# An encoder block's opening on one core: squares summed over channels by the tensor engine, first scale read from PSUM, last tile's products bank by bank

## Chip, cores, metric

One NeuronCore of a Trainium2 chip runs the whole program. The metric is device time in microseconds (us); lower is better. The engines are named as the profile names them: PE (tensor engine), ACT (scalar engine), DVE (vector engine), POOL (GpSimd), SP (the queue that issues most transfers).

## What is computed

One layer of a streaming-encoder block, x of 512 tokens by 1024 channels: a half-step SwiGLU FFN, a mixer (indexed sparse attention beside an RG-LRU branch), a second half-step FFN. Each sub-layer is RMSNorm, adaLN shift and scale from c, the sub-layer, RMSNorm, adaLN gate, residual. The change is in the first sub-layer's start:

```python
mod = (jax.nn.silu(c) @ w_ada[l] + b_ada[l]).reshape(B, N_MOD, D)
h = modulate(rmsnorm(x, ffn1_pre_g[l]), m[0], m[1])    # x * rsqrt(mean(x*x) + eps) * g, then h*(1+scale)+shift
y = swiglu(h, ffn1_w_gate[l], ffn1_w_up[l], ffn1_w_down[l])
x = x + 0.5 * m[2][:, None, :] * rmsnorm(y, ffn1_post_g[l])
```

## The kernel before

Activations stand transposed: channels on the 128 partitions, eight channel tiles of 128, and 512 tokens along the row. A weight W and an activation h are each split into a high part, rounded for PE's fast fp32 form, and a low remainder; a product is three matmuls per 128 channels (Whi·hhi, Whi·hlo, Wlo·hhi). `split` (L213) makes the parts: ACT copies the raw tile to hi (L217), DVE subtracts to lo (L221). Raw tiles come through a ring of three (`raw`), hi and lo through rings of six.

`start` (L511) is the opening. SP issues x in four transfers, the identity, then in turn the first adaLN weights (`wa`) and the first FFN weights (`w0`, one load for each of the eight channel tiles, each for three gate and three up column blocks). The order of PE's work in it is written out by hand (`manual_schedule`), and so is SP's order in the whole program; ACT, DVE and POOL, and PE outside the opening, follow a scheduler that simulates the program and issues what it holds to be ready.

- `busy(n)` (L571) puts n dummy 128x128 products of ones on PE.
- The sum of squares: ACT squares each tile of x (L620), DVE adds the eight (L624, L626) into one tile, PE sums its channels with four one-column matmuls (L630), ACT takes the root (L631), DVE the reciprocal (L632), PE spreads it over the partitions by four transposes (L636), and ACT copies that scale from PSUM to SBUF as `r` (L638).
- `mod_rows(g)` (L577) multiplies silu(c) by a group of adaLN weights, as rows of one partition (L585), `mod_cols(g)` (L589) turns the rows to columns (L594), adds the bias, and makes hi and lo of h for the tiles of the group (L603 to L605). `prepare(g)` (L607) splits the group's weights and makes u = x·r (L612).
- Then eight tiles k follow. For each, 18 products (L672) go to six PSUM banks (three gate, three up blocks): six Whi·hhi, six Wlo·hhi, six Whi·hlo. All six banks close in the last tile.
- `act_tile` (L675) makes silu(gate)·up: Silu on ACT (L679), product on DVE (L680), then hi and lo (L682, L683). The next weight tiles' products (L316 to L318) need the banks that it releases.

Four `mm` banks, two `wo` and two `aux` share PSUM. ACT loads a table set before a function that the present set lacks (ACT_TABLE_LOAD); `warm` (L562) is a one-element Sqrt that only loads the Sqrt set early. Later, `presplit` (L258) splits more weights in the background by way of POOL's transfers (L273 to L275), and `boundary` (L405) goes from one sub-layer to the next: `rstd_steps` (L321) sums squares on PE (L330), takes the reciprocal root on DVE by Newton steps (L336 to L348) or on ACT, and spreads it by transposes (L356); the second FFN then starts half by half of the tokens, with products at L310, L311 and L313 that take the low part of h last.

Of the kernel before, what the change touches and what calls it, by code (L numbers as in the profile page):

```python
# [9 lines left out]
AF = mybir.ActivationFunctionType  # L10
ALU = mybir.AluOpType
# [3 lines left out]
P = 128  # L15
S = 512
D = 1024
ND = D // P
# [14 lines left out]
NSTART = 3  # L33
# [77 lines left out]
class Build:  # L111
# [399 lines left out]
    def start(self):  # L511
        nc = self.nc
# [9 lines left out]
        w0 = [None] * ND  # L522
# [38 lines left out]
        warm = c.tile([P, 1], F32, name="warm")  # L561
# [9 lines left out]
        def busy(n):  # L571

            for _ in range(n):
                nc.tensor.matmul(idle[:, :P], self.ones, self.ones, start=True, stop=True)
# [14 lines left out]
        def mod_cols(g):  # L589

            pt = rows[g % 2]
            k0, n = groups[g][0], len(groups[g])
            for q in range(2 * n):
                nc.tensor.matmul(pt[:, q:q + 1], accs[g][:, q * P:(q + 1) * P], self.sel, start=True, stop=True)  # L594
            mk = self.modc[:, :16].rearrange("p (j d) -> p d j", d=8)[:, k0:k0 + n]
            bk = self.col("b_ada", 0, 16).rearrange("p (j d) -> p d j", d=8)[:, k0:k0 + n]
            nc.vector.tensor_tensor(mk, pt[:, :2 * n].rearrange("p (d j) -> p d j", j=2), bk, op=ALU.add)
            gm = self.modc[:, 8 + k0:8 + k0 + n]
            nc.vector.scalar_tensor_tensor(gm, gm, 1.0, self.col("g1pre", k0, n), op0=ALU.add, op1=ALU.mult)
            for k in groups[g]:  # L600
                gamma, beta = self.modc[:, 8 + k:9 + k], self.modc[:, k:k + 1]
                h32 = self.w2("h32")
                nc.scalar.activation(hi[k], us[k], AF.Identity, scale=gamma, bias=beta)  # L603
                nc.scalar.activation(h32, us[k], AF.Identity, scale=gamma, bias=beta)
                self.late = nc.vector.tensor_tensor(lo[k], h32, hi[k].bitcast(F32), op=ALU.subtract)  # L605

        def prepare(g):  # L607

            for k in groups[g]:
                self.split(w0[k])  # L610
                us[k] = self.w2("u")
                nc.vector.tensor_tensor(us[k], self.X[k], r, op=ALU.mult)  # L612

        with self.tc.manual_schedule(engines={mybir.EngineType.PE}):
            busy(34)

            totals = []
            for k in range(ND):
                sq = self.w2("sq")
                nc.scalar.activation(sq, self.X[k], AF.Square)  # L620
                if k < 2:
                    totals.append(sq)
                else:
                    nc.vector.tensor_tensor(totals[k % 2], totals[k % 2], sq, op=ALU.add)  # L624
            total = totals[0]
            nc.vector.tensor_tensor(total, total, totals[1], op=ALU.add)  # L626
            pt = self.bank("wo")
            s, s2 = [self.small.tile([P, 4], F32, name="s", tag="s4") for _ in range(2)]
            for q in range(4):
                nc.tensor.matmul(pt[:, q:q + 1], total[:, q * P:(q + 1) * P], self.ones[:, 0:1], start=True, stop=True)  # L630
            nc.scalar.activation(s, pt[:, :4], AF.Sqrt, bias=self.eps, scale=1.0 / D)  # L631
            nc.vector.reciprocal(s2, s)  # L632
            pb = self.bank("wo")
            mod_rows(0)
            for q in range(4):
                nc.tensor.transpose(pb[:, q * P:(q + 1) * P], s2[:, q:q + 1].to_broadcast([P, P]), self.ident)  # L636
            r = self.w2("r")
            nc.scalar.activation(r, pb, AF.Copy)  # L638
            prepare(0)
            mod_cols(0)  # L640
            mod_rows(1)
            busy(4)
            prepare(1)
            banks = [self.bank("mm") for _ in range(4)] + [self.bank("wo") for _ in range(2)]
            for gi, g in enumerate(groups):
                for k in g:
                    if k + 3 < ND:
                        fetch_w(k + 3)
                    if k < 2:
                        fetch(k + 3)  # L650
                    for part in range(3):
                        for j in range(2 * NSTART):
                            self.first_product(banks[j], w0[k], j, k, part)

                        if part == 0 and k == g[-1] and gi + 1 < len(groups):
                            mod_cols(gi + 1)
                    self.alive -= 1

                    if k == g[0]:
                        nx = gi + 2 if gi == 0 else gi + 1  # L660
                        if gi != 1 and nx < len(groups):
                            mod_rows(nx)
                            prepare(nx)
                    if k >= 6:
                        self.feed(k - 5)
# [728 lines left out]
```

## Time and profile before

| | |
|---|---|
| median of 3 runs | 1077.83 us (1075.47 to 1077.92) |
| the profiled execution | 1078.11 us, its span 1076.3 us |
| PE busy | 1047.9 us (97%) |
| DVE, ACT, POOL busy | 639.9 us, 481.5 us, 81.3 us |
| mean granted clock of PE | 0.984 |
| moved from and to HBM | 188.52 MB read, 23.61 MB written |

The span runs from the first to the last instruction; the execution's own time is 1.8 us longer. A granted clock of 1.00 is 2.4 GHz, 0.50 is 1.2 GHz. An fp32 matmul (dummies, sums, transposes) stands as two records in PE's rows, a product of split parts as one. In a timeline row the columns are start, duration, engine, line, operation, output<-input, tile sizes and the number of instructions merged; in brackets stands the engine's idle time before it and what ended that.

### The profile page before, as it was taken

How to read it: one execution, taken by the hardware profiler on the slowest of the kernel's cores; microseconds unless marked ns; L12 is line 12 of the kernel's file. 1: busy time of each engine (PE TensorE's matmuls, PEld its weight loads, DVE VectorE, ACT ScalarE, POOL GpSimd, SP SyncE). 2: the span in 40 equal slices, each digit the busy share in tenths (PEclk: the TensorE clock that was granted, in tenths of full speed). 3: DMA queues.
4: the chain of work that ended last, by engine and by line, in shares of the span. 5: the costliest groups of instructions: out<-in, count | busy, mean ns of one | idle time of the engine just before them, and what ended most of it. 6: DMA issues, size and time to landing. Idle time of an engine off the chain costs nothing.

```text
span 1076.3 us, 15177 instructions
## 1 busy us (share of the span) xinstructions
PE 1047.9 (97%) x5860; PEld 889.3 (83%) x5860; DVE 639.9 (59%) x1189; ACT 481.5 (45%) x779; POOL 81.3 (8%) x148
## 2 busy tenths in 40 slices
PE   8989999999999999999999999899999999999996
PEld 6778888878888999997776578899988888888895
DVE  4578578676866246479997555876423333333345
ACT  5564244333333356455876654554333222222252
POOL 0001111010111000000212410000000000000000
PEclk8999999999999999999999999899999999999998
DMA  9688898988989669583535412242433323333212
GB/s 369 262 329 288 296 350 308 335 287 305 369 296 369 236 218 336 205 325 117 200 128 168 149 42 79 79 138 88 148 118 98 93 86 100 114 98 98 98 41 79
DMA packets 56184, 211.03 MB, mean 196 GB/s; under 512 B 6936, under 2 KB 9304, under 8 KB 51504
## 3 DMA queue, kind: packets, MB, share of 16 engines
q1 hardware_dynamic: 42208, 161.72, 43.1%
q0 software_dynamic: 13904, 48.35, 12.6%
q8 instruction: 46, 0.75, 0.3%
q14 instruction: 26, 0.21, 0.1%
HBM read 188.52 MB, written 23.61 MB: 197 GB/s over the span
## 4 chain that ended last, share of the span: by engine, by line
PE 87%; DMA 5%; DVE 3%; ACT 3%; issue 2%; SPq 0%; DVEq 0%; ACTq 0%; POOLq 0%
PE mm L316 13%; PE mm L317 13%; PE mm L318 12%; PE wo L317 8%; PE wo L316 8%; PE wo L318 8%; PE mm L310 3%; PE mm L311 3%; PE mm L313 3%; DMA pre<-in_win_dram 2%; PE mm L1207 2%; PE wo L310 1%; PE wo L311 1%; PE wo L313 1%; PE aux L1244 1%
## 5 line engine op out<-in xcount | busy, mean ns | idle before, releaser
L217 ACT ACTIVATE hi<-raw 128x1024 fp32r<-128x1024 f32 (+2 forms) x192 | 196.8, 1029 | 304.6 <-PE mm L317 129.3
L221 DVE TENSOR_TENSOR lo<-raw,hi 128x1024 fp32r<-128x1024 f32 (+2 forms) x151 | 177.8, 1181 | 124.4 <-ACT hi L217 123.4
L316 PE MATMUL mm<-hhi,hi 128*128 128x512 f32 x368 | 144.9, 394 | 3.4 <-ACT sg L679 3.4
L318 PE MATMUL mm<-hhi,lo 128*128 128x512 f32 x368 | 143.8, 391 | 0.0
L317 PE MATMUL mm<-hlo,hi 128*128 128x512 f32 x368 | 143.7, 391 | 0.0
L316 PE MATMUL mm<-ahi,hi 128*128 128x256 f32 (+1 forms) x330 | 109.9, 334 | 1.0 <-ACT ahi L682 1.0
L316 PE MATMUL wo<-hhi,hi 128*128 128x512 f32 x280 | 110.0, 393 | 0.0
L317 PE MATMUL mm<-alo,hi 128*128 128x256 f32 (+1 forms) x330 | 109.9, 333 | 0.0
L318 PE MATMUL mm<-ahi,lo 128*128 128x256 f32 (+1 forms) x330 | 109.8, 333 | 0.0
L318 PE MATMUL wo<-hhi,lo 128*128 128x512 f32 x280 | 109.6, 391 | 0.0
L317 PE MATMUL wo<-hlo,hi 128*128 128x512 f32 x280 | 109.5, 391 | 0.0
L316 PEld LDWEIGHTS mm<-hhi,hi 128*128 128x128 f32 x368 | 69.5, 189 | 18.0 <-ACT sg L679 3.8
L318 PEld LDWEIGHTS mm<-hhi,lo 128*128 128x128 f32 x368 | 69.4, 189 | 14.6
L317 PEld LDWEIGHTS mm<-hlo,hi 128*128 128x128 f32 x368 | 69.6, 189 | 14.2
L456 DVE SCALAR_TENSOR_TENSOR macc<-wa,cs,macc 128x512 f32<-128x512 f32 x98 | 73.5, 750 | 5.2 <-DMA wa<-in_wa_dram 3.1
L273 ACT ACTIVATE pre<-pre 128x1024 fp32r<-128x1024 f32 x33 | 34.9, 1059 | 77.4 <-DMA pre<-in_win_dram 53.1
L316 PEld LDWEIGHTS mm<-ahi,hi 128*128 128x128 f32 x330 | 62.5, 190 | 7.4 <-ACT ahi L682 1.4
L317 PEld LDWEIGHTS mm<-alo,hi 128*128 128x128 f32 x330 | 62.7, 190 | 6.2 <-DVE alo L683 0.2
L318 PEld LDWEIGHTS mm<-ahi,lo 128*128 128x128 f32 x330 | 62.7, 190 | 6.0
L317 PEld LDWEIGHTS wo<-hlo,hi 128*128 128x128 f32 x280 | 52.6, 188 | 11.5 <-issue 0.7
L316 PEld LDWEIGHTS wo<-hhi,hi 128*128 128x128 f32 x280 | 52.6, 188 | 11.5 <-issue 0.5
L318 PEld LDWEIGHTS wo<-hhi,lo 128*128 128x128 f32 x280 | 52.6, 188 | 11.3 <-issue 0.5
(264 smaller groups left out, 2012.0 us busy)
## 6 DMA issues: line engine op xcount, KB each, us to landing
raw<-in_gu_dram SPq DMA_DIRECT2D x89, 512.0 KB, 3.6
wa<-in_wa_dram SPq DMA_DIRECT2D x36, 1024.0 KB, 10.0
lo<-pre SPq DMA_DIRECT2D x41, 512.0 KB, 5.2
pre<-pre POOLq DMA_DIRECT2D x33, 512.0 KB, 8.7
raw<-in_dn_dram SPq DMA_DIRECT2D x32, 448.0 KB, 3.5
raw<-in_win_dram SPq DMA_DIRECT2D x26, 512.0 KB, 5.7
raw<-in_dn_dram SPq DMA_DIRECT2D x22, 512.0 KB, 4.6
pre<-in_win_dram POOLq DMA_DIRECT2D x21, 512.0 KB, 5.0
```

The lines of the kernel that those rows point to most:

```text
L217: nc.scalar.activation(l.hi, l.raw, AF.Copy)
L221: nc.vector.tensor_tensor(l.lo, l.raw, l.hi.bitcast(F32), op=ALU.subtract)
L273: nc.scalar.activation(hi.bitcast(F32R), raw, AF.Copy)
L310: self.nc.tensor.matmul(ps, l.hi[:, kt], xh[kt][:, tok], start=(q == 0), stop=False)
L311: self.nc.tensor.matmul(ps, l.lo[:, kt], xh[kt][:, tok], start=False, stop=False)
L313: self.nc.tensor.matmul(ps, l.hi[:, kt], xl[kt][:, tok], start=False, stop=(q == n - 1))
L316: self.nc.tensor.matmul(ps, l.hi[:, kt], xh[kt][:, tok], start=(q == 0), stop=False)
L317: self.nc.tensor.matmul(ps, l.hi[:, kt], xl[kt][:, tok], start=False, stop=False)
L318: self.nc.tensor.matmul(ps, l.lo[:, kt], xh[kt][:, tok], start=False, stop=(q == n - 1))
L456: nc.vector.scalar_tensor_tensor(acc, w[:, k], ck, acc, op0=ALU.mult, op1=ALU.add)
L1207: nc.tensor.matmul(ps[:, :n], self.q[rows, g, i * P:(i + 1) * P], self.k[rows, g, :n], start=True, stop=False)
L1244: nc.tensor.matmul(ps[64 * e:64 * e + 64, :P], self.v[:, t, 64 * h:64 * h + 64], pts[e][:, t * P:(t + 1) * P], start=(t == 0), stop=(t == i))
```

## The change

The squares are no longer added by DVE: each squared tile goes to PE at once, which adds its channels into one PSUM column per 128 tokens over eight rounds, with four dummy products between rounds; the dummies ahead are 16 in place of 34. The first tile's u is made from the PSUM bank with the transposed scale, and the copy to `r` comes after it. In the last of the eight tiles all 18 products go bank by bank, three for each, and a one-element Silu stands ahead of them in the program.

```diff
         with self.tc.manual_schedule(engines={mybir.EngineType.PE}):
-            busy(34)
-
-            totals = []
+            busy(16)
+
+            pt = self.bank("wo")
             for k in range(ND):
                 sq = self.w2("sq")
                 nc.scalar.activation(sq, self.X[k], AF.Square)
-                if k < 2:
-                    totals.append(sq)
-                else:
-                    nc.vector.tensor_tensor(totals[k % 2], totals[k % 2], sq, op=ALU.add)
-            total = totals[0]
-            nc.vector.tensor_tensor(total, total, totals[1], op=ALU.add)
-            pt = self.bank("wo")
+                for q in range(4):
+
+                    nc.tensor.matmul(pt[:, q:q + 1], sq[:, q * P:(q + 1) * P], self.ones[:, 0:1],
+                                     start=(k == q == 0), stop=(k == ND - 1), skip_group_check=True)
+                if k < ND - 1:
+                    busy(4)
             s, s2 = [self.small.tile([P, 4], F32, name="s", tag="s4") for _ in range(2)]
-            for q in range(4):
-                nc.tensor.matmul(pt[:, q:q + 1], total[:, q * P:(q + 1) * P], self.ones[:, 0:1], start=True, stop=True)
             nc.scalar.activation(s, pt[:, :4], AF.Sqrt, bias=self.eps, scale=1.0 / D)
...
+            r = pb
+            prepare(0)
+            mod_cols(0)
             r = self.w2("r")
             nc.scalar.activation(r, pb, AF.Copy)
-            prepare(0)
-            mod_cols(0)
             mod_rows(1)
...
-                    for part in range(3):
+                    if k == ND - 1:
+
+                        nc.scalar.activation(warm, self.cs[:, 0:1], AF.Silu)
+                        for j in range(2 * NSTART):
+                            for part in range(3):
+                                self.first_product(banks[j], w0[k], j, k, part)
+                    for part in range(3 if k < ND - 1 else 0):
                         for j in range(2 * NSTART):
                             self.first_product(banks[j], w0[k], j, k, part)
```

Lines behind the opening move down by four (L679 is L683 in the changed kernel). What the scheduler makes of it shows in the order of the instructions. ACT's order from the first Silu on, before:

```order
L560 ACTIVATE cs<-cols 128x8
L562 ACT_TABLE_LOAD
L562 ACTIVATE warm<-cs,eps 128x1
L620 ACTIVATE sq<-X_116 128x512 x4
L620 ACTIVATE sq<-X_117 128x512 x4
L631 ACTIVATE s<-wo,eps 128x4
L217 ACTIVATE hi<-raw 128x768
```

and in the changed kernel:

```order
L560 ACTIVATE cs<-cols 128x8
L562 ACT_TABLE_LOAD
L562 ACTIVATE warm<-cs,eps 128x1
L651 ACT_TABLE_LOAD
L651 ACTIVATE warm<-cs 128x1
L620 ACTIVATE sq<-X_116 128x512 x4
L620 ACTIVATE sq<-X_117 128x512 x4
L217 ACTIVATE hi<-raw 128x768 x2
L628 ACT_TABLE_LOAD
L628 ACTIVATE s<-wo,eps 128x4
```

The one-element Silu (L651) stands ahead of the squares; two splits and a table load stand between the squares and the root (L628).

ACT's order at the end of the opening, from the last activations of h on (`lt` belongs to the decay branch of the mixer), before:

```order
L604 ACTIVATE h_514<-u,modc 128x512
L217 ACTIVATE hi<-raw 128x1024 x2
L273 ACTIVATE pre<-pre 128x1024
L982 ACT_TABLE_LOAD
L982 ACTIVATE lt_616<-lt_615 128x4
L217 ACTIVATE hi<-raw 128x1024 x2
L679 ACT_TABLE_LOAD
L679 ACTIVATE sg<-mm 128x512
```

and in the changed kernel:

```order
L604 ACTIVATE h_545<-u,modc 128x512
L217 ACTIVATE hi<-raw 128x1024 x2
L683 ACT_TABLE_LOAD
L683 ACTIVATE sg<-mm 128x512
L986 ACT_TABLE_LOAD
L986 ACTIVATE lt_648<-lt_647 128x4
L683 ACT_TABLE_LOAD
L683 ACTIVATE sg<-mm 128x512
L683 ACTIVATE sg<-wo 128x512
```

Two of the four splits (L217, 128x1024) have moved ahead of the last activations of h, and the decay branch's load now stands between the first and the second Silu.

PE's order in the second FFN, at the end of the first half of the tokens, where the root for the second half is made, before:

```order
L310 MATMUL wo<-hhi_6314,hi 128x256
L330 MATMUL aux<-ones,ssum 128x1 x4
L311 MATMUL wo<-hhi_6314,lo 128x256
...
L313 MATMUL wo<-hlo_6316,hi 128x256 x4
L313 MATMUL wo<-hlo_6317,hi 128x256 x4
L356 MATMUL aux<-ident,s 128x128 x2
L310 MATMUL mm<-hhi_6314,hi 128x256
```

and in the changed kernel:

```order
L311 MATMUL wo<-hhi_6347,lo 128x256
L313 MATMUL wo<-hlo_6348,hi 128x256 x4
L313 MATMUL wo<-hlo_6349,hi 128x256 x4
L330 MATMUL aux<-ones,ssum 128x1 x4
L356 MATMUL aux<-ident,s 128x128 x2
L310 MATMUL mm<-hhi_6346,hi 128x256
```

The sums (L330) stood 17 matmuls ahead of the transposes (L356), and now stand right in front of them.

## Rows read from the trace of the kernel before

**Rows 1.** The page's first part: busy us (share of the span), instructions.
```profile
PE 1047.9 (97%) x5860; PEld 889.3 (83%) x5860; DVE 639.9 (59%) x1189; ACT 481.5 (45%) x779; POOL 81.3 (8%) x148
```

**Rows 2.** Timeline of ACT, from 0 to 13 us.
```profile
4.27 0.29 ACT L562 ACTIVATE warm<-cs,eps 128x1 f32<-128x1 f32 x1
5.58 3.71 ACT L620 ACTIVATE sq<-X 128x512 f32<-128x512 f32 x6 [1.02 <-DMA X<-in_x_dram]
9.52 1.15 ACT L620 ACTIVATE sq<-X 128x512 f32<-128x512 f32 x2 [0.23 <-DVE sq L624]
```

**Rows 3.** Timeline of PE, from 12 to 27 us.
```profile
12.26 1.05 PE L630 MATMUL wo<-ones,sq 128*128 128x1 f32 x8 [1.83 <-DVE sq L626]
13.25 1.04 PE L585 MATMUL aux<-wa,cs 128*1 128x256 f32 x16
...
17.62 2.08 PE L574 MATMUL mm<-ones 128*128 128x128 f32 x8
19.34 2.05 PE L672 MATMUL mm<-hhi,hi 128*128 128x512 f32 x4
...
25.04 1.90 PE L585 MATMUL aux<-wa,cs 128*1 128x512 f32 x16
```

**Rows 4.** Windows of PE: stretch, length, PE busy (records), granted clock, DMA share, GB/s.
```profile
4.60:5.60 1.00, 1.00 (x12) 1.00 1.08 397
4.60:10.30 5.70, 5.70 (x53) 1.00 1.03 405
14.60:17.60 3.00, 3.00 (x23) 0.50 1.02 419
17.60:21.30 3.70, 3.70 (x17) 0.50 1.00 405
25.04:28.30 3.26, 3.26 (x23) 1.00 0.98 403
437.81:441.20 3.39, 2.45 (x20) 1.00 0.22 49
441.25:444.60 3.35, 3.35 (x16) 0.50 0.51 178
```

**Rows 5.** Timeline of PE at the end of the opening.
```profile
62.08 0.61 PE L672 MATMUL wo<-hlo,hi 128*128 128x512 f32 x2
66.12 0.80 PE L316 MATMUL mm<-hhi,hi 128*128 128x512 f32 x1 [3.42 <-ACT sg L679]
...
69.23 0.39 PE L317 MATMUL mm<-hlo,hi 128*128 128x512 f32 x1
...
71.50 0.39 PE L318 MATMUL mm<-hhi,lo 128*128 128x512 f32 x1
```

**Rows 6.** Timeline of ACT at the same place.
```profile
63.10 1.06 ACT L217 ACTIVATE hi<-raw 128x1024 fp32r<-128x1024 f32 x1 [2.15 <-DMA raw<-in_gu_dram]
64.17 1.28 ACT L679 ACT_TABLE_LOAD   x1
65.47 0.60 ACT L679 ACTIVATE sg<-mm 128x512 f32<-128x512 f32 x1
```

**Rows 7.** Timeline of PE in the second FFN.
```profile
724.96 0.95 PE L330 MATMUL aux<-ones,ssum 128*128 128x1 f32 x8
725.76 0.36 PE L311 MATMUL wo<-hhi,lo 128*128 128x256 f32 x1
...
729.17 0.41 PE L356 MATMUL aux<-ident,s 128*128 128x128 f32 x2 [1.13 <-DVE s L348]
```

**Rows 8.** DMA issues between 5.64 and 6.10 us: KB, us to landing.
```profile
raw<-in_w_dram SPq DMA_DIRECT2D x1, 384.0 KB, 10.9
```

**Rows 9.** Timeline of DVE in the second FFN.
```profile
725.94 0.16 DVE L336 TENSOR_SCALAR s<-aux 128x2 f32<-128x2 f32 x1 [1.98 <-PE aux L330]
...
728.87 0.16 DVE L348 SCALAR_TENSOR_TENSOR s<-s 128x2 f32<-128x2 f32 x1
```

**Rows 10.** Waits of PE over the span: us in total, times, longest.
```profile
PE mm L316 <- ACT ahi L682: 1.0, 1, 1.0
```

## The prediction

> **What bounds the kernel now.** I read the busy line of the page first. The tensor engine (PE) is busy for 97% of the span [rows 1], so time moves only where PE waits, runs at its lower clock, or does work that is no product. The change touches three such places, each read in the timelines of PE, ScalarE (ACT) and VectorE (DVE).
>
> The first is the opening. ACT squares the eight 128x512 tiles of x as their transfers land, from 5.58 to 10.67 us [rows 2]; DVE adds them up, and PE, idle for 1.83 us until it has, needs one set of four matmuls for the channel sums, from 12.26 to 13.31 [rows 3]. From there PE is the chain: adaLN rows, transposes and dummy products stand back to back until the first real product at 19.34, mostly at 1.2 GHz, the granted clock being 0.50 from 14.60 to 21.30 [rows 3, 4].
>
> The second is the end of the opening. The last product of the eight tiles starts near 62.3, and PE then stands idle for 3.42 us until the first Silu has released a bank; ACT was held by a split that waited for a weight transfer, and then by a 1.28 us table load [rows 5, 6]. After the gap PE runs at half speed until 69.2.
>
> The third is a place that the diff doesn't name: the middle of the second FFN's split half, where PE waits 1.13 us for the last reciprocal root [rows 7].
>
> **The change, part by part.**
>
> *Squares summed by PE.* DVE's seven adds go. In their place come 28 more one-column matmuls, in eight rounds of four, and dummy products of four between the rounds; the 34 dummies at the start become 16. Each fp32 matmul is two records. A dummy's record costs 0.112 us at 2.4 GHz (4.70 us more of window hold 41 more records, with one more at the edge, [rows 4]), a one-column record about the same, 8 being issued between 12.26 and 13.25, 0.12 each at most [rows 3]. So a round is 0.9 us and its dummies 0.9 us. All rounds and gaps together are 64 + 56 = 120 records, 13.4 us. ACT delivers a square every 0.6 us, so PE is the slower one, and the dummies, meant to bridge waits, come on the path.
>
> When can it begin? The order of ACT's instructions shows that the scheduler has put the new Silu load not ahead of the last tile but right behind the first Sqrt load. The Sqrt warm-up ends at 4.56 [rows 2]; a load of 1.28 and a short activation bring the first square to about 6.05, 0.5 later than now, and PE's first round to 6.7. PE's 16 dummies end near 6.3, so nothing else holds it. The sums are complete at 6.7 + 13.4 + 0.15 = 20.25 in place of 13.31: **+6.9**. Lower bound: at the 0.10 per record of the same kind of sum inside the product stream (8 records between 724.96 and 725.76, [rows 7]) the rounds shrink by 0.7, +6.2. Upper bound: everything at 1.2 GHz, where 8 records take 1.72 [rows 3], 25.8 in place of 13.4, +19.3. I take 2.4 GHz, because half of the mixed stretch is dummies: the stretch from 25.04 to 28.30, of which 1.9 us are one-row adaLN products and the rest real ones, kept clock 1.00, while the one from 437.81, with PE busy for 2.45 of 3.39 us, was followed by the lower clock [rows 3, 4].
>
> *New table load before the square root.* Silu's set being loaded, the Sqrt comes back with 1.28 us, behind two splits of weight tiles. The second tile lands about 16.6 (10.9 us after its issue at about 5.7) [rows 8], so split and load end near 18.8, before the sums at 20.25: nothing, as long as the squares are the later ones. If PE were done at 13.3 as now, this queue would cost 5 us.
>
> The load's price has a page in the Trainium skill, "ScalarE: Activation LUTs", section "What ACT_TABLE_LOAD costs": a load plus a drain, 2.66 us for each switch. The trace disagrees, its Silu starting 1.30 us after the load's start [rows 6]. By the page the squares and PE's rounds would begin 1.4 later, and the sum would be 1083.4.
>
> *First scale from PSUM, copy later.* DVE reads the transposes directly, and the copy (0.6 us, as the Silu of that size [rows 6]) goes behind the first tile's activations. PE's own chain is the bound between the sums and the first product, so I count nothing; the bank that the copy still reads is the sixth to be written, over a microsecond after the first. Bounds: -0.6 to +0.6, the copy itself either way.
>
> *The chain from sums to products* is as now, 6 us, with its stay at 1.2 GHz: when the rounds end, the same adaLN rows, transposes and one-column products follow. It shifts as a whole.
>
> *Last tile bank by bank.* The 18 products cost the same. The first bank closes 15 products, 3.4 us, before the last (0.227 each, ten starts from 69.23 to 71.50, [rows 5]). ACT's order now has the splits of the weight tiles earlier, so their ring slots and transfers come earlier; behind the last split stand a Silu load (the early one is lost to the Sqrt), the first Silu, a load for the decay branch, and Silu once more. Load and first Silu, 1.28 + 0.60 [rows 6], fit in the 3.4. The gap goes: 66.12 against 62.53, when the next product would have started, is **-3.6**; with no gap there is no lower clock, under which seven starts took 3.11 (66.12 to 69.23) where 1.59 is the normal price: **-1.5** [rows 5]. Bounds: -5.1, and 0 if the wait for the transfer at 63.06 stays. Late next are second and third Silu, whose banks PE wants 5 and 11 us later.
>
> *Second FFN.* The order shows PE's last channel sum of the mixer's boundary moved behind the last products of the first half, right in front of the transposes that need its root. Now 17 matmuls stand between, and cover 2.3 (725.76 to 728.04, which is 729.17 less 1.13) of the 3.1 us that DVE takes from reading the sums (725.94) to the last Newton step (729.03) [rows 7, 9]. In the changed order the products end 0.8 earlier, the sums at 728.2, the root near 731.2, and the transposes start at 731.3 against 729.17: **+2.1**. Bounds: +1.5 with nothing interleaved on DVE; +3.5 if the longer wait also lengthens the stay at 1.2 GHz.
>
> *Other queues.* SP's order is unchanged. On ACT, DVE and POOL the pre-split tiles of later weights change places with their neighbours; the products of the first FFN hide that now but for one wait of 1.0 us on PE [rows 10], and I leave it at nothing, between -1.0 and +1.0, should that wait go or come twice.
>
> Sum: 6.9 - 5.1 + 2.1 = +3.9 on the profiled execution's 1078.11 (span 1076.3 and 1.8 around it; it lies 0.3 above the median of 1077.83): **1082.0 us**. A difference under 0.3%, 3.2 us, can't be told from none here.
>
> **The rivals.**
>
> *A. The clock holds.* The new opening leaves PE hardly an idle moment until the first product. If only idle time lowers the clock, the 6.7 us at 1.2 GHz [rows 4] run at 2.4, and give back 3.35: 1078.6, not slower. Against it: PE showed no idle time between 12.26 and the fall at 14.6, and it stayed low to 17.60 though PE was busy throughout [rows 3, 4]. The Trainium skill's "TensorE: Matmul & The Clock Gate", section "Why this matters for your kernels", says this rule: leave no idle gaps between bursts of matmuls and the clock stays. The rows agree for the gap at 62.7, not for the second half of the first stay. Chance 0.15.
>
> *B. The clock falls amid the rounds.* From the middle of the rounds, near 13.4, the remaining 6.8 us then double: 1088.8; from 11 on it would be 1091. For it: the fall at 14.6 came behind such one-column matmuls; against it: the stretch at 25.04 [rows 3, 4]. Chance 0.17.
>
> *C. The gap stays.* If the last weight transfer is again late against the end of the products, ACT reaches its load late, and 1.5 to 5 us of the gain don't come: 1083.5 to 1087. It needs a landing after the first bank's closing; splits moved ahead speak against it. Chance 0.10.
>
> *D. The rounds hide.* If the weight loads of a round slip under the dummies' streaming, the two don't add, the rounds cost 13.4 - 6.3, and the sum is -2.4: 1075.7; with A as well 1072.4. For it: PE's loads overlap its matmuls. Against it: one-column records in a stream still took 0.10 each [rows 7]. Chance 0.13.
>
> **How the numbers follow.** The forecast holds 0.45, within 1080.5 to 1083.5; about 0.28 of it lies above the bound of 1081.06, 0.17 below. Slower: 0.28 + 0.17 (B) + 0.10 (C) = 0.55. Same: 0.17 + 0.13 of A + 0.06 of D = 0.36. Faster: 0.02 + 0.07 = 0.09. Range 1076.0 to 1089.0: it leaves out the lower half of D and the worse form of B. The likeliest case's own range is 1080.5 to 1083.5.
>
> **What would show it.** Sums right: the last one-column record of the opening ends near 20.2, the first product starts near 26.2. Right on the load: two table loads before the squares and one more before the root, PE never waiting for it. End: no gap between the last tile's products and the next weight tile, clock 1.00 there. Second FFN: an idle stretch of 3 us before the transposes in place of 1.13. The forecast is wrong if the sums end before 16 or after 24, or if the gap is still over a microsecond.

## The result, and the profile after

| | before | changed |
|---|---|---|
| median (runs) | 1076.65 us (4, 1070.96 to 1077.92) | 1089.68 us (4, 1089.49 to 1090.34) |
| the profiled execution, its span | 1078.11 us, 1076.3 | 1089.49 us, 1087.7 |

The changed kernel is slower: 1.0125 times, 95% interval 1.0093 to 1.0157, of which 1 is no part. Slower was forecast, but 1082.0 us, and 1089.68 lies just outside the range that ended at 1089.0. The spans differ by 11.4 us where +3.9 was expected, so 7.5 us came from somewhere else.

The busy line of the page after answers to [rows 1]: PE's share is the same 97%, and it is busy for 8.7 us longer.

```profile
PE 1056.6 (97%) x5934; PEld 898.8 (83%) x5936; DVE 636.1 (58%) x1182; ACT 485.2 (45%) x783; POOL 81.7 (8%) x148
```

**The opening, as far as the first product.** PE's timeline after, against [rows 3] (L623 are the sums, L574 the dummies, L676 the products that were L672):

```profile
7.08 0.95 PE L623 MATMUL wo<-ones,sq 128*128 128x1 f32 x8
7.89 1.14 PE L574 MATMUL mm<-ones 128*128 128x128 f32 x8
...
19.59 0.95 PE L623 MATMUL wo<-ones,sq 128*128 128x1 f32 x8
20.47 1.04 PE L585 MATMUL aux<-wa,cs 128*1 128x256 f32 x16
...
24.50 1.17 PE L676 MATMUL mm<-hhi,hi 128*128 128x512 f32 x4
```

The rounds and their dummies alternate without a gap, and the sums end at 20.54 (19.59 + 0.95) in place of 13.31, 7.2 later. But the first product comes 4.0 us after that, not 6.0: the adaLN rows and transposes ran at full clock. ACT's timeline, against [rows 2], shows the Silu load ahead of the squares and the Sqrt load back before the root, both hidden: the second load is done at 20.03, and the sums end at 20.54.

```profile
4.56 1.28 ACT L651 ACT_TABLE_LOAD   x1
...
5.96 3.21 ACT L620 ACTIVATE sq<-X 128x512 f32<-128x512 f32 x6
...
18.75 1.28 ACT L628 ACT_TABLE_LOAD   x1
20.58 0.26 ACT L628 ACTIVATE s<-wo,eps 128x4 f32<-128x4 f32 x1 [0.54 <-PE wo L623]
```

**Three places behind it.** PE's timeline after, at the last adaLN columns of the opening, at its end [rows 5], in the first FFN, and in the second [rows 7]:

```profile
57.80 1.87 PE L594 MATMUL aux<-sel,macc 128*128 128x1 f32 x8 [2.69 <-ACT macc L587]
...
72.44 0.39 PE L676 MATMUL wo<-hlo,hi 128*128 128x512 f32 x1
72.67 0.39 PE L316 MATMUL mm<-hhi,hi 128*128 128x512 f32 x1
...
244.90 0.73 PE L316 MATMUL mm<-ahi,hi 128*128 128x512 f32 x1 [4.01 <-ACT ahi L686]
...
739.13 0.40 PE L356 MATMUL aux<-ident,s 128*128 128x128 f32 x2 [2.89 <-DVE s L348]
```

At 72.67 the gap of 3.42 us is gone, as forecast. The other three are what to look at: a wait of 2.69 that did not exist, one of 4.01 where 0.97 stood (the 1.0 of [rows 10]), and 2.89 in place of 1.13. Windows of PE give the clock (columns as in [rows 4], but with all five engines' busy time ahead of it: PE, PEld, DVE, ACT, POOL):

```profile
6.00:20.54 14.54, 14.54 (x135) 14.53 (x137) 1.92 (x2) 7.36 (x12) 0.00 (x0) 1.00 1.02 412
20.54:24.50 3.96, 3.95 (x48) 2.39 (x49) 1.14 (x4) 1.98 (x4) 0.00 (x0) 1.00 1.04 419
...
57.27:64.09 6.82, 6.29 (x19) 5.33 (x20) 3.38 (x5) 4.20 (x6) 1.08 (x2) 0.50 1.00 371
...
245.00:248.41 3.41, 3.41 (x8) 2.65 (x9) 2.32 (x3) 1.23 (x2) 0.54 (x1) 0.50 0.81 290
...
739.93:746.76 6.83, 6.12 (x28) 6.12 (x29) 6.03 (x16) 3.34 (x8) 0.00 (x0) 0.50 0.01 2
```

Behind each of the three waits PE then works at 0.50 for a while. At 57 and at 245 it loses half of that stay, as it has work nearly throughout. In the second FFN it loses less, since part of the stay is idle time: run 6, further down, has the same stay of 6.8 us, run 5 has none, and the stay costs run 6 about 1.8 us. The difference of the spans is made up of these: first six products, +4.2 (the next record, the adaLN columns, starts at 25.98 against 21.74); wait and clock at 57, 2.7 + 3.4, +6.1; end of the opening, -5.1; wait and clock in the first FFN, 4.0 - 1.0 + 1.7, +4.7; a stay at 0.50 in the mixer that no longer occurs (the last of [rows 4]), -1.7; second FFN, +2.8 (the same products of PE start at 724.24 and 732.53 ahead of its wait, 8.3 later, and at 751.00 and 762.12 behind its stay, 11.1 later). Together +11.0, against 11.4; what is left is in small shifts, the largest one of 0.5 near 120 us.

**Where the new waits come from.** ACT copies `macc`, PE's adaLN rows, out of PSUM. ACT's timeline after:

```profile
56.20 1.06 ACT L273 ACTIVATE pre<-pre 128x1024 fp32r<-128x1024 f32 x1 [3.43 <-DMA pre<-in_dn_dram]
57.16 0.58 ACT L587 ACTIVATE macc<-aux 128x512 f32<-128x512 f32 x1
...
243.28 1.06 ACT L273 ACTIVATE pre<-pre 128x1024 fp32r<-128x1024 f32 x1 [7.99 <-DMA pre<-in_wv_dram]
244.24 0.61 ACT L686 ACTIVATE ahi<-a 128x512 fp32r<-128x512 f32 x1
```

Both times ACT stood in front of a pre-split copy (L273), waiting for POOL's transfer of that weight tile, and what PE wanted was queued right behind. The chain of waits runs through it (start, length, what):

```profile
46.48 3.60 DMA pre<-pre
...
50.10 0.02 POOLq L266
50.12 0.50 issue
...
50.63 5.46 DMA pre<-in_dn_dram
...
56.20 1.06 ACT pre L273
57.26 0.49 ACT macc L587
57.75 0.04 issue
57.80 1.87 PE aux L594 x8
```

In the kernel before a copy stood ahead of that `macc` too, but it was the second tile's. POOL had issued its load at 44.41, ahead of the first tile's write, and ACT waited 1.1 us for it, unseen by PE. Now the write goes first, and the copy ahead of `macc` is the third tile's (run 7 ties just this one). `presplit` has two buffers that it takes in turn, so the third tile's load goes to the buffer that the first tile's write reads. POOL's queue waits for that write, which lands at 50.08, and the load is issued at 50.63; the second tile's load comes right behind it. The x tiles in the other buffer came free at nearly the same time (50.04), but only the second tile's load needs them.

### The profile page after: what moved, and what is told of

Same layout as the page of the kernel before. It is cut to its first block, busy times and chain, and to the rows that moved or that the text cites. A ratio compares the mean times of both kernels' runs of the same rounds, so it can differ in the third digit from the quotient of the medians.

```text
span 1087.7 us, 15322 instructions
## 1 busy us (share of the span) xinstructions
PE 1056.6 (97%) x5934; PEld 898.8 (83%) x5936; DVE 636.1 (58%) x1182; ACT 485.2 (45%) x783; POOL 81.7 (8%) x148
## 4 chain that ended last, share of the span: by engine, by line
PE 79%; DMA 11%; DVE 4%; ACT 2%; issue 2%; DVEq 0%; POOL 0%; SPq 0%; ACTq 0%; POOLq 0%
PE mm L316 10%; PE mm L317 10%; PE mm L318 10%; PE wo L317 7%; PE wo L316 7%; PE wo L318 7%; DMA pre<-pre 5%; DMA pre<-in_win_dram 3%; PE mm L310 3%; PE mm L311 3%; PE mm L313 3%; PE mm L1211 2%; PE mm L676 1%; PE wo L310 1%; PE wo L311 1%
## 5 line engine op out<-in xcount | busy, mean ns | idle before, releaser
L217 ACT ACTIVATE hi<-raw 128x1024 fp32r<-128x1024 f32 (+2 forms) x192 | 197.0, 1029 | 292.2 <-PE mm L317 100.8
L316 PE MATMUL mm<-hhi,hi 128*128 128x512 f32 x368 | 144.1, 392 | 0.0
L316 PE MATMUL mm<-ahi,hi 128*128 128x256 f32 (+1 forms) x330 | 110.6, 336 | 4.0 <-ACT ahi L686 4.0
L316 PE MATMUL wo<-hhi,hi 128*128 128x512 f32 x280 | 109.9, 393 | 0.0
L318 PEld LDWEIGHTS mm<-hhi,lo 128*128 128x128 f32 x368 | 69.1, 188 | 14.6
L317 PEld LDWEIGHTS mm<-hlo,hi 128*128 128x128 f32 x368 | 69.1, 188 | 14.1
L316 PEld LDWEIGHTS mm<-hhi,hi 128*128 128x128 f32 x368 | 69.1, 188 | 14.0
L273 ACT ACTIVATE pre<-pre 128x1024 fp32r<-128x1024 f32 x33 | 34.9, 1059 | 92.7 <-DMA pre<-in_win_dram 46.5
L316 PEld LDWEIGHTS mm<-ahi,hi 128*128 128x128 f32 x330 | 62.8, 191 | 10.5 <-ACT ahi L686 4.4
L274 DVE TENSOR_TENSOR pre<-pre 128x1024 fp32r<-128x1024 f32 x33 | 40.3, 1223 | 41.0 <-ACT pre L273 41.0
L310 PE MATMUL mm<-hhi,hi 128*128 128x256 f32 x232 | 60.9, 294 | 1.2 <-ACT hhi L373 1.1
```

Source lines behind the costliest of these rows:

```text
L217: nc.scalar.activation(l.hi, l.raw, AF.Copy)
L273: nc.scalar.activation(hi.bitcast(F32R), raw, AF.Copy)
L274: nc.vector.tensor_tensor(raw.bitcast(F32R), raw, hi, op=ALU.subtract)
L310: self.nc.tensor.matmul(ps, l.hi[:, kt], xh[kt][:, tok], start=(q == 0), stop=False)
L316: self.nc.tensor.matmul(ps, l.hi[:, kt], xh[kt][:, tok], start=(q == 0), stop=False)
L317: self.nc.tensor.matmul(ps, l.hi[:, kt], xl[kt][:, tok], start=False, stop=False)
```

## Experiments

**The theory:** the loss beyond the rounds is the scheduler's new order, set off by the squares' edit: the pre-split's loads, writes and copies on POOL and ACT, and the sums in the second FFN. **Its rivals:** the waits come from the other parts (the scale in PSUM, the early Silu, bank by bank), or from PE's lateness or busy transfers, whatever the order.

The kernel before was run beside each group of runs; its median was 1076.0 to 1076.5 us beside runs 1 to 11. Single runs of one kernel differ by several us (those of the kernel before lay between 1068 and 1085), so the ratios carry the verdicts on time and the traces those on places. The table gives, for each profiled execution, how much later than in the kernel before (us) the same five records of PE start (the last one: ends): the first product, the first product of the next weight tile (L316, the end of the opening), the first product with `ahi` (first FFN's second weight), the first with `mhi` (end of the mixer), and PE's last record.

| | first product | next tile | first `ahi` | first `mhi` | last | ratio of times, interval |
|---|---|---|---|---|---|---|
| changed | +5.2 | +6.6 | +5.0 | +8.3 | +11.4 | 1.0125 (1.0093 to 1.0157) |
| 1 squares alone | +4.7 | +2.2 | +0.9 | +10.9 | +14.1 | 1.0150 (1.0114 to 1.0187) |
| 2 DVE squares | +0.1 | -1.8 | -3.2 | -3.7 | -3.7 | 0.9962 (0.9933 to 0.9990) |
| 3 pre-split held | +4.9 | +1.0 | -0.4 | +4.6 | +4.6 | 1.0086 (1.0058 to 1.0115) |
| 4 rounds bare | +5.4 | +2.3 | +0.9 | +5.4 | +5.9 | 1.0054 (1.0021 to 1.0087) |
| 5 40 dummies | -1.4 | -4.1 | -5.5 | -8.2 | -8.4 | 0.9953 (0.9931 to 0.9975) |
| 6 41 dummies | -1.2 | -4.6 | -6.0 | -6.1 | -4.6 | 0.9981 (0.9955 to 1.0008) |
| 7 one copy later | +5.0 | +6.6 | +5.1 | +7.3 | +5.3 | 1.0042 (1.0021 to 1.0063) |
| 8 one dummy | +4.7 | +1.7 | +0.3 | +0.6 | +3.4 | 1.0083 (1.0055 to 1.0111) |
| 9 dummies alone | -0.9 | -2.0 | -1.8 | -3.1 | -5.0 | 0.9983 (0.9962 to 1.0005) |
| 10 bank and dummies | +0.7 | -2.4 | -3.8 | -5.5 | -5.9 | 0.9969 (0.9941 to 0.9996) |
| 11 38 dummies | +1.1 | -2.6 | -4.0 | -7.0 | -6.9 | 0.9972 (0.9945 to 0.9998) |

**1. Squares alone.** The squares' part of the diff, put into the kernel before, and nothing else.

> The kernel before with one part of the change: squares summed by PE in eight rounds with dummies. Theory (the extra time comes from the squares' edit: the rounds on PE's path, and the new order that the scheduler makes of it; the other parts don't move the order): sums complete near 20.0, first product near 24.2 at full clock; the wait of PE for the copied adaLN rows (macc) near 56 comes as in the changed kernel, 2.7 us and 3.3 of lower clock behind it; the second FFN costs 3.5 as there; the end of the opening keeps a gap of 1 to 3.4 us. 1083 to 1092 us, likeliest 1088. Rival (the waits come from reading the scale in PSUM, the early Silu or the bank-by-bank tile): only the rounds cost, 1080 to 1081, and no macc wait.

Measured: 1092.63 us. The theory's cause holds, its place only in part. PE waited 1.07 us for `macc` with no lower clock behind it, but three times in the first FFN (2.9, 1.9 and 3.5 us, for `ahi` and `alo`; ahead of the first ACT had waited 5.7 us in a pre-split copy), with 10.2 us at 0.50; the second FFN has its 2.9 us. So the squares' edit alone brings about the whole loss (the two intervals overlap), in an order of its own. The rival's 1080 is excluded. Unexpected: the gap at the end of the opening shrank to 0.5 us without the bank-by-bank order, ACT having done the decay branch's load earlier. PE's products there go from 5.2 us late to 0.9 us late, so 4.3 of the 5.1 us come without that part of the change.

**2. The other parts without the squares.** The changed kernel with these lines back:

```diff
-            busy(16)
+            busy(34)
...
-                for q in range(4):
-                    nc.tensor.matmul(pt[:, q:q + 1], sq[:, q * P:(q + 1) * P], self.ones[:, 0:1],
-                                     start=(k == q == 0), stop=(k == ND - 1), skip_group_check=True)
-                if k < ND - 1:
-                    busy(4)
+                if k < 2:
+                    totals.append(sq)
+                else:
+                    nc.vector.tensor_tensor(totals[k % 2], totals[k % 2], sq, op=ALU.add)
...
```

> The changed kernel with the squares added by DVE again; PSUM scale, bank-by-bank tile and early Silu stay. Theory: the order behind the opening is that of the kernel before, so no macc wait, 1.0 us of wait at the first FFN, 1.1 in the second; the end of the opening gains its 5.1; two table loads more in the opening cost at most 0.5. 1071 to 1073.5 us, about 4.5 below the kernel before. Rival (these three parts bring the waits, or gain nothing): 1077 or more.

Measured: 1072.27 us, faster than both kernels, as the theory has it. POOL's order and PE's are those of the kernel before, no wait for `macc`, 1.13 us in the second FFN.

**3. The order alone, first way.** The changed kernel, with the first two pre-split copies of ACT tied behind its last activation of h (`self.h32` is that instruction, and `issue_after` puts what is written in its block behind it on the same engine):

```diff
-            nc.scalar.activation(hi.bitcast(F32R), raw, AF.Copy)
+            with self.tc.issue_after(self.h32.ins) if k < 2 else contextlib.nullcontext():
+                nc.scalar.activation(hi.bitcast(F32R), raw, AF.Copy)
```

> The changed kernel with one thing added: ACT's first two pre-split copies are ordered behind its last activation of the opening's h. Theory (ACT stood in a pre-split copy that waited for its transfer, with macc queued behind): the macc wait near 56 and the lower clock behind it go, -6.0; in the second FFN the sums stand 20 matmuls ahead of the transposes again, -3.5; the wait of 4 us near 241, of the same kind, may stay or go (-4.7). 1075 to 1081 us. Rival (PE late by the rounds, or the transfers' contention, makes those waits whatever the order): a wait of over a microsecond stays before the adaLN columns near 56, 1087 to 1091.

Measured: 1084.82 us, 1082.76 in the profiled execution. The rival falls: with PE just as late (+4.9 at the first product), no wait stands before the columns near 55, the clock is 1.00 from the rounds to 346 us, and the wait near 241 is down to 0.6. At the first `ahi` product the kernel is 0.4 ahead of the one before, where the changed kernel is 5.0 behind. The second FFN's wait is 1.1 again. But the time is above the expected range, since other waits come with the delayed pre-split (lines lie two lower here); the one at L492, which run 4 with the same copies held has too, is followed by 3.4 us at 0.50:

```profile
PE aux L492 <- DVE macc L458: 3.1, 1, 3.1
...
PE wo L318 <- ACT ahi L688: 1.9, 1, 1.9
```

**4. Rounds without dummies.** No `busy(4)` between the rounds, no early Silu, ACT's opening in program order, the copies held as in 3.

> The changed kernel without the dummies between the rounds and without the early Silu, ACT's opening in program order, the first two pre-split copies held as in the third run. Theory: PE's eight rounds of 0.9 us follow ACT's squares and end near 14.0, little later than DVE's way; if the clock holds from there to the first product, as it does in the changed kernel, 3 us less than before, with the end of the opening's 5.1: 1068 to 1071 us; if it falls as in the kernel before, 1071 to 1074. Rival (the dummies are what holds the clock): the lower clock lies over the adaLN rows as in the kernel before.

Measured: 1083.43 us; a miss on the opening, and the rival is right. Windows of this run, from the first round to the end of the sums (columns as above):

```profile
6.00:10.21 4.21, 4.21 (x37) 4.21 (x35) 0.00 (x0) 3.44 (x6) 0.00 (x0) 1.00 1.03 389
10.21:18.46 8.25, 8.25 (x41) 8.23 (x41) 0.00 (x0) 1.15 (x2) 0.00 (x0) 0.50 1.02 420
```

PE is busy throughout, with nothing but one-column sums from 7.42 on, and the clock falls at 10.21 and stays low until 23.87. The sums end at 18.5, 2 us earlier than with the dummies, and the first product is the latest of all. The dummies are not idle weight: with four of them between rounds the clock held in the rounds, in the changed kernel and in runs 1, 3 and 7, and without them it fell.

**5 and 6. Idle time, and one dummy more.** The kernel before with scale from PSUM and bank by bank, DVE's squares, and only the number of leading dummies changed:

```diff
-            busy(34)
+            busy(40)
```

(41 in run 6.)

> The kernel before with the first scale from PSUM and the last tile bank by bank, DVE adding the squares, no early Silu, and 40 dummies ahead in place of 34; the order of the other engines is that of the kernel before. PE's idle time ahead of the sums shrinks from 1.95 to about 0.6 us. Theory (that idle time let the clock fall at 14.6): the clock stays 1.00 to the first product, which starts near 16.4 in place of 19.4: 1068 to 1070 us. Rival (the one-column sums, one-row products and transposes let it fall, whatever came ahead): it falls near 14.6 again, first product at 19.4, 1071 to 1073 us as in the second run.

> The fifth run with one dummy product more, 0.22 us of PE's work in its idle time, by which the scheduler puts the second FFN's sums right ahead of their transposes and, in the opening, a weight split ahead of the root. Theory (the order alone makes the second FFN's loss): 2.9 us of wait in place of 1.1 there, and 6.8 us at the lower clock in place of 3.4, +3.5 against the fifth run, and 0.3 to 0.5 for the split: 3 to 4.5 us slower than the fifth. Rival (the loss comes with the late start of the changed kernel): the two agree within 1 us.

Measured: 1070.73 and 1074.44 us. Run 5 has the lowest ratio of all, 0.9953 of the kernel before, though the intervals of runs 2, 10 and 11 overlap its own. PE's timeline of run 5 shows no idle time ahead of the sums, and the first product 5.3 us after their start instead of 7.1:

```profile
1.01 11.74 PE L574 MATMUL mm<-ones 128*128 128x128 f32 x80 [1.01 <-POOL sel L555]
12.66 1.05 PE L630 MATMUL wo<-ones,sq 128*128 128x1 f32 x8
...
17.93 1.17 PE L677 MATMUL mm<-hhi,hi 128*128 128x512 f32 x4
```

The clock stays 1.00 until 661.7 us; the stays at the end of the opening, at 441 in the mixer and behind the 1.13 us of wait in the second FFN are gone with it. Run 6 adds one dummy of 0.2 us, and the second FFN's sums change place as in the changed kernel. The same line of PE's timeline, of run 5 and of run 6:

```profile
722.26 0.41 PE L356 MATMUL aux<-ident,s 128*128 128x128 f32 x2 [1.13 <-DVE s L348]
```

```profile
724.24 0.66 PE L356 MATMUL aux<-ident,s 128*128 128x128 f32 x2 [2.89 <-DVE s L348]
```

With it come 6.8 us at 0.50 (722.84 to 729.67), where run 5 has none: PE's transposes start 2.0 us later than in run 5, its products behind the stay 3.8 us later. From the last `mhi` product to the end run 6 loses 3.1 us against run 5 (1059.31 - 675.99 against 1063.13 - 676.69). No late start of PE is needed for that loss; a different order is enough. A further 2 us comes from a wait behind ACT in the first FFN, at 230.

**7. The order alone, second way.** The changed kernel with just the third tile's copy, the one ahead of `macc`, tied behind it (k == 2 and `macc` in place of k < 2 and `h32`).

> The changed kernel with one instruction ordered: ACT's pre-split copy of the third tile, which stood ahead of the last macc, has to follow it. Theory: the wait of 2.7 us near 55 and the 6.8 us of lower clock behind it go, -6.0; the second FFN's sums stand 21 matmuls ahead of the transposes again by the scheduler's new order, -3.5; two copies now stand ahead of the last four activations of h and may hold them for their transfers, 0 to 2 us; the wait of 4 us near 241 may stay or go. 1076 to 1083 us. Rival (late PE or busy transfers make the wait): over 1 us of wait stays at the adaLN columns near 55, 1087 or more.

Measured: 1081.66 us. The wait before the columns is gone, the second FFN is back at 1.1 us, and the time is in the range. But the two copies that now stand ahead of the last h hold PE there; the trace has it as (lines two lower):

```profile
PE mm L678 <- ACT hhi L605: 4.2, 1, 4.2
PE mm L318 <- ACT ahi L688: 3.4, 1, 3.4
```

0 to 2 us were expected, so this was underestimated: the wait moved to the next thing in ACT's queue, since the transfer itself is no earlier, and 3.4 us at 0.50 came with it. The 3.4 in the first FFN also stays.

**8. One dummy between rounds.** `busy(1)` for `busy(4)`, ACT's opening in program order, no early Silu, second and third copy held.

> The changed kernel with one dummy between the rounds in place of four, without the early Silu, ACT's opening in program order, the second and third pre-split copy held behind the opening's last activation. For the opening's clock: if a quarter of a microsecond of dummies in every 1.2 is enough, the clock stays at 1.00 and the sums end near 16.3, the first product near 20; if not, it falls amid the rounds as in the fourth run, sums near 20. The rest of the program as in the third and fourth runs, 1076 to 1084 us.

Measured: 1086.9 us (1081.53 profiled), above the range. The clock fell at 11.50, PE without a gap from 6.41 on, and the sums ended at 18.43. One dummy product in each round is not enough here; four were.

**9 to 11. Parts, once more.** Run 9 is the kernel before with 40 dummies and nothing else; run 10 adds the bank-by-bank tile, without the scale from PSUM; run 11 is run 5 with 38 dummies.

> The kernel before with 40 dummies ahead in place of 34, and nothing else. Theory (the fill holds the clock in the opening; only the last tile's bank-by-bank order closes the gap at the opening's end): no stay at 1.2 GHz from 14.6 to 21.4, first product 1.0 to 1.8 us earlier, but the gap of 3.4 us before the next weight tile stays within a microsecond, with its lower clock: 1073 to 1075 us. Rival (the gap goes when ACT and its transfers shift against PE, without the new order): 1071 or less.

> The fifth run without the scale read from PSUM: the copy to r comes first again, as in the kernel before. Theory (that scale is worth nothing, since PE's own chain is the bound there): within 0.7 us of the fifth run, 1070 to 1071.5. Rival (the copy of 0.6 us was on the path once PE runs at full clock): first product 0.6 later than in the fifth run, or more.

> The fifth run with 38 dummies ahead in place of 40: about 0.5 us more of idle time ahead of the sums. If that much idle time is harmless, the clock stays 1.00 through the opening and the time is within 0.5 us of the fifth run, 1070 to 1071.5; if not, it falls near 14.6 again and the time is 1071.5 to 1073.

Measured: 1074.23, 1072.79 and 1070.95 us. The first product of the next weight tile, of run 9 and of run 10:

```profile
64.12 0.80 PE L316 MATMUL mm<-hhi,hi 128*128 128x512 f32 x1 [3.21 <-ACT sg L679]
```

```profile
63.67 0.50 PE L316 MATMUL mm<-hhi,hi 128*128 128x512 f32 x1 [0.62 <-ACT sg L683]
```

The bank-by-bank edit closes most of the gap here, and with it goes the stay at 0.50 from 64.08 to 67.49. But the bank's earlier closing is not what did it. ACT's timeline of run 10:

```profile
61.73 1.28 ACT L683 ACT_TABLE_LOAD   x1
63.02 0.60 ACT L683 ACTIVATE sg<-mm 128x512 f32<-128x512 f32 x1
63.52 1.05 ACT L217 ACTIVATE hi<-raw 128x1024 fp32r<-128x1024 f32 x1
```

The first Silu starts right behind its table load, when even the tile's last product has started (62.66). What moved it is ACT's order: the split that waited 2.15 us for its transfer ahead of that load [rows 6] now stands behind the Silu, at 63.52. This too is the scheduler's order, set off by an edit. Run 10 is no test of the scale, because its clock fell; runs 5 and 9, both at 1.00, are: the first product starts 5.27 and 5.30 us after the sums, with and without it. The four windows from 14.55 to 20.00 us, of runs 5, 9, 10 and 11 in turn (the granted clock is the third number from the end):

```profile
14.55:20.00 5.45, 5.13 (x45) 3.50 (x41) 3.60 (x7) 3.58 (x7) 0.00 (x0) 1.00 1.03 420
```

```profile
14.55:20.00 5.45, 5.22 (x51) 3.39 (x44) 3.65 (x8) 4.14 (x7) 0.00 (x0) 1.00 1.04 425
```

```profile
14.55:20.00 5.45, 5.45 (x37) 3.75 (x33) 3.25 (x7) 3.68 (x7) 0.00 (x0) 0.50 1.02 419
```

```profile
14.55:20.00 5.45, 5.45 (x38) 3.36 (x31) 2.97 (x6) 3.37 (x6) 0.00 (x0) 0.50 1.04 425
```

PE's idle time ahead of the sums was 0, 0.51, 0.99 and 1.63 us in these four. With the first two the clock held, with the others it fell at 14.5, as it did with 1.83 in the kernel before and 1.95 in run 2; what PE does after the idle time is the same in all. But runs 5 and 9 had also first risen to 1.00 later, at 6.4 and 6.1 in place of 4.2 and 4.3, which is what made their dummies end later. In run 11 the opening came as the second arm of its expectation has it, the time as the first: it made up for it behind, with no gap at all at the end of its opening. Run 10 is 2.1 us above run 5, a miss; the fall of the clock is in its profiled execution, but run 11 had it too and was as fast as run 5, so it does not explain the difference by itself.

**12 to 18. Idle time or the moment of the rise?** The kernel before with 48 leading dummies (no idle time) and with 28 (over 2 us), in several executions, since the moment of the first rise differs from one to the next (a dummy's record takes 0.21 us before it, 0.11 after). Beyond that nothing is changed.

> The kernel before with 48 leading dummies, so many that PE has no idle time ahead of the sums however late the clock first rises. Only the opening is read. So far the clock held where that idle time was 0 to 0.51 us, and there it had also first risen late (6.0 to 6.4), and fell where it was 0.99 to 1.95, and there it had risen early (4.2 to 4.3). Theory (the idle time decides): it holds to the first product, risen early or late. Rival (the moment of the rise decides, and the work on sums, rows and transposes brings it down): it falls near 14.5 if it rose near 4.3, and holds if it rose after 6.

> The kernel before with 28 leading dummies: over 2 us of idle time ahead of the sums, risen early or late. Only the opening is read. Theory (the idle time decides): the clock falls before the first product in any case. Rival (the moment of the rise): it falls near 14.5 if it rose near 4.3, and holds if it rose after 6.

> The twelfth run once more, for another moment of the rise, since that differs between executions: the same two answers.

> The thirteenth run once more, for another moment of the rise: the same two answers.

> 28 dummies a third time. The runs with 28 fell, having risen at 4.8 and 4.9; those with 48 held, having risen at 6.1 and 6.8. If this one rises after 5.4: the theory (idle time decides) has it fall before the first product all the same, the rival (moment of the rise) has it hold.

> 28 dummies a fourth time, for another moment of the rise: the same two answers.

> 48 dummies a third time. If this one rises before 5: the theory (idle time decides) has it hold to the first product, the rival (moment of the rise) has it fall near 14.5.

| run | dummies | first rise to 1.00 | idle ahead of the sums | in the opening | time of the one execution |
|---|---|---|---|---|---|
| 12, 14, 18 | 48 | 6.1, 6.8, 6.9 | 0 | held, in all three | 1080.06, 1076.62, 1077.29 |
| 13, 15 | 28 | 4.9, 4.8 | 2.70, 2.65 | fell at 11.7, 11.6 | 1085.69, 1088.99 |
| 16, 17 | 28 | 6.4, 6.7 | 2.37, 2.20 | fell at 13.3, 13.5 | 1080.24, 1090.95 |

Runs 16 and 17 rose as late as those that held, and fell: the late rise does not save the clock, the idle time decides there. The rise still moves the moment of the fall: 11.6 to 11.7 after the early ones, 13.3 to 13.5 after the late ones. The other half, an early rise without idle time, did not come up with 48 dummies. The nearest is run 1, which rose at 4.4 and had the rounds in place of the idle time: it held through the same rows and transposes.

These runs show something more. With 28 dummies the kernel before, its squares still added by DVE and its first product between 0.5 earlier and 1.6 later, has the changed kernel's trouble. The waits of PE in run 13:

```profile
PE mm L316 <- ACT ahi L682: 5.9, 1, 5.9
PE aux L356 <- DVE s L348: 3.2, 1, 3.2
...
PE mm L672 <- ACT hhi L603: 2.5, 1, 2.5
```

They lie at 237 us, in the second FFN, and at 56 us. In ACT's order two pre-split copies now stand ahead of the last h. Six dummies fewer at the start, and nothing else, bring these waits; neither squares on PE nor a late PE is needed. Against the one trace of the kernel before, PE's last record comes 2 to 13 us later, but these are single executions, so the waits carry the point and not the times. The other direction is not free of it either: run 12, with 48, waits 2.6 us for `ahi` and 3.2 in the second FFN.

## Why the prediction was wrong

Point by point, by its own steps:

- **Squares summed by PE, +6.9:** right. The rounds and gaps took the forecast's 13.4 us within 0.1 (7.08 to 20.54), the sums came 7.2 later, and the clock held in them. Rival D (rounds hide under the dummies) did not come about, nor did B, though runs 4 and 8 show how near it was: with none or one of the four dummies the clock falls in the rounds.
- **Table load before the root, first scale from PSUM, 0:** right, both (20.03 before 20.54; 5.27 against 5.30).
- **"The chain from sums to products is as now, 6 us, with its stay at 1.2 GHz":** wrong, by -3.0. What rival A forecast came about here. The prediction argued against it that PE had no idle time between 12.26 and the fall at 14.6, and overlooked the 1.83 us that ended at 12.26. Runs 12, 14 and 18 against 16 and 17 show it for idle times of 2.2 to 2.4 us: without them the same rows and transposes run at 1.00, with them they don't, at the same moment of the first rise. For the 1.83 of the kernel before, with its early rise, it is a conclusion from these and from run 1, which rose as early, had no idle time and held. The rule of the Trainium skill's "TensorE: Matmul & The Clock Gate", section "Why this matters for your kernels", that gaps between bursts of matmuls bring the clock down, agrees with these in its direction, though the gaps here are shorter than those it warns of. It is not the whole: in runs 4 and 8 the clock fell with PE busy throughout, on one-column sums.
- **Last tile bank by bank, -5.1:** the size right, 5.1; the gap and the lower clock behind it went. But most of that is ACT's new order and not the bank's early closing: run 1 gains 4.3 of it without this part, and in run 10 (4.2 against run 9) the first Silu did not need the early closing.
- **Second FFN, +2.1:** mechanism and wait right (2.89), the size a little small, +2.8. The stay at 0.50 doubled, 6.8 us for 3.4, as the upper bound of +3.5 has it, but part of it was idle. Run 6 shows wait and stay together, with one dummy as the only edit.
- **"Other queues ... I leave it at nothing, between -1.0 and +1.0":** this step failed. The changed places of the pre-split tiles cost +6.1 at 57 us and +4.7 in the first FFN, 10.8 in all. The order of POOL's loads and writes and of ACT's copies was there to be read, and so was the wait of ACT for such transfers; what was missing was to ask, for each copy that ACT meets ahead of something that PE needs, when its load can be issued. Run 3 shows that with these copies elsewhere both waits go, run 2 that without the squares they don't arise, and the runs with 28 dummies that the order brings them without the squares.

The forecast's sum, put right, is 7.2 - 3.0 - 5.1 + 2.8 + 10.8 - 1.7 (the stay in the mixer that did not come, of which no step spoke) = +11.0. Two errors of opposite sign, -3.0 and +10.8, stood behind a right direction. That the direction came true was luck: without the 10.8 that the prediction put at nothing, the rest of this sum comes to +0.2.

What stays open: why the scheduler turns the orders at these points (41 dummies, not 40; 28, not 34); whether 1.0 to 1.8 us of idle time would let the clock fall after a late rise too; and how the stays at 0.50 late in the program, as in the mixer, come and go between kernels.

## What to carry to other kernels

Where a scheduler sets the order, an edit of the opening is also an edit of every place behind it: compare the orders of all engines, and follow each transfer that an in-order engine meets ahead of work on the critical path back to its issue and to the release of its buffer. One dummy product cost 3 us behind the mixer this way, and tying a single copy moved its wait to the next instruction in the queue rather than removing it. An idle stretch of PE can cost twice, once as itself and once at the lower clock behind it. One-column work in its place did not hold the clock here without four dummy products between the rounds, and those were then on the path.

## What the runs showed of the hardware

PE's clock fell in two ways that the traces keep apart: within an idle stretch of 1.0 us or more, or up to 2.3 us behind its end, PE being busy again; and amid one-column matmuls without any idle time (at 10.21 with no dummies between them, at 11.50 with one product in each round, not at all with four). Not every such stretch brings it: behind the 1.13 us in the second FFN the clock fell in the kernel before, at 731.36, and stayed at 1.00 in runs 5, 7 and 9. A round of eight one-column records takes 0.95 us at 1.00 and 1.71 at 0.50. The stay behind a wait is not the longer the longer the wait: 6.8 us after waits of 2.7 and 2.9, 3.4 after 4.0 and 4.2. And the moment when the clock first rises differs between executions of one program, 4.8 to 6.7 us in the four with 28 dummies, and from 4.2 to 6.9 over all runs; 40 leading dummies took 10.8 to 11.7 us in three of them.
